# Seven products of half blocks for five channel groups of a gated mixer, projection B ahead of A, gate rows behind the heads

## The chip, the cores and the metric

The kernel runs on one core of a Trainium2 chip as one launch. The metric is device time in microseconds, the median of several runs. Engines are named as in the profile: PE or TensorE (matmuls), PEld (its weight loads), DVE or VectorE, ACT or ScalarE, POOL or GpSimd, SP or SyncE (which issues nearly all DMAs).

## The reference: one step of a hybrid decoder layer

One layer for 1024 prompt rows and 8 sample rows, D = 1024, all in float32. Cut to what matters:

```python
mod = silu(c) @ ada_w + ada_b
shift, scale, gate = split(mod, 3)
h = rmsnorm(x, norm_pre) * (1 + scale) + shift
proj = h @ w_in                                   # 10256 columns
hA, cA, bA, zA, qkv, zB, beta, alpha, gA, gB = split(proj)
a_conv, new_buf_a = causal_dwconv(cA * hA, buf_a, conv_a_w)      # width 3
yA = ((bA * a_conv) * silu(zA)) @ w_out_a
q, k, v = split(silu(causal_dwconv(qkv, buf_b, conv_b_w)))       # width 4, then l2norm of q, k
o, S = gated_delta_chunked(q, k, v, sigmoid(beta), g(alpha), s0) # 8 heads of 128
yB = (rmsnorm(o, onorm_w) * silu(zB)) @ w_out_b
merged = sigmoid(gA) * yA + sigmoid(gB) * yB
y = x + gate * rmsnorm(merged @ w_o, norm_post)
```

The outputs are y for both groups of rows, the last rows of both convolutions and the delta-rule states.

## The kernel before

Activations lie transposed: channels on the 128 partitions, 1032 tokens (`NT`: 1024 of the prompt, 8 of the samples) along the free dimension. Every float32 operand of a large matmul is split into a rounded high part and the remainder (type float32r), and a product is three matmuls: high x high, high x low, low x high. The input h lies in `xh` and `xl` (128 x 8 x 1032 each) from the start to the end of the input projection.

The work of TensorE is an ordered list, `jobs`. A job makes 128 output channels for all tokens: three groups of 344 tokens (`GROUPS`), each 8 k-tiles of three matmuls into one PSUM bank, so 72 matmuls. The job's weights are loaded two jobs ahead (`w_load`, 512 KB on SP) and split one job ahead (`w_split`: two casts on ScalarE, two subtractions on VectorE). After each group `evac` empties the bank. The order of the list before: for each of 8 heads the jobs k, q, v, up to two gate jobs and z; then for each of 8 channel groups of branch A the jobs h, c, b, z (`branch_a_jobs`); two late gate jobs; 8 jobs of projection A (`w_out_a`), 8 of projection B (`w_out_b`). Behind the list comes the tail, `merged @ w_o` with norm and residual by 128 rows.

Everything else (the delta rule of a head, the sample rows, the gate rows, loads and splits for the projections) is written as generators, "strands". A planner of its own, `Sched`, adds up planned costs of every instruction on each engine while the program is written. `slot()`, called after every k-tile, lets each strand take its next step once its planned time and a slack of 450 ns (`SLK`) have been reached by TensorE's planned clock; `force(cond)` moves that clock on and lets strands step until `cond` holds. The planner thereby fixes the order of instructions in each engine's queue and nothing else: on the chip every queue runs in order and waits on semaphores.

Names that the change touches:

- `rowgate_gen`: the `gate` part of the modulation, by 8 column blocks of 128: load, cast, remainder, 16 matmuls. It is started ahead of job 3, so in the heads, and holds three of the five buffers `T4`.
- `T4`, `MT` (`Slots`): numbered buffers, taken and given back first in, first out.
- `yAsc`, `yBsc`, `gAsc`, `gBsc`: DRAM scratch for the branch outputs and the gates.
- `to_outputs`, before the fourth channel group: waits for all strands, releases the heads' pool `bp`, and loads and splits the first three yA rows (`load_split`); later groups write their split output straight into `ya`.
- `to_out_a`, `to_out_b`: at the start of the projections `xh`, `xl` are released, `mrg`, `yb` and `wo` allocated, loads started.

The hooks that tie these together:

```python
hook(3, lambda: start(rowgate_gen()))
hook(iga + 4 * GRP_SW, to_outputs)
hook(ioa, to_out_a)
hook(iob, to_out_b)
```

## Time and profile before

| | |
|---|---|
| median of 3 runs | 1485.18 us (1481.81 to 1486.23) |
| the profiled execution | 1483.92 us, its span 1482.2 us |
| mean granted TensorE clock | 0.987 |
| busy share of the span: PE, DVE, ACT, POOL | 98%, 57%, 41%, 2% |
| instructions | 24892, of them 9890 matmuls |
| DMA | 133.14 MB, mean 90 GB/s |

All instructions are recorded by a helper, so every row of the profile has the line L121; groups are told apart by tile names (`pm_t<-xh,whi` is a matmul of the job list into PSUM, `pa_t` a small matmul of a strand, `wlo<-wraw,whi` a weight remainder). Matmuls overlap in the record, so a matmul's cost is the distance of starts. Groups of rows stand by engine, operation, tiles and shape with count, busy us and mean ns of one, and behind the bar the idle time of the engine just before and who ended it.

### The profile page before, as it was taken

Reading aid. Unit: us, or ns where it says so; the run is one execution under the profiler, and the core shown is the slowest. Engines: PE = TensorE matmul, PEld = TensorE weight load, DVE = VectorE, ACT = ScalarE, POOL = GpSimd, SP = SyncE. Lnnn points to the kernel's source line nnn. Section 1 sums busy time; section 2 is a strip of 40 time slices with the busy share of each in tenths; the row PEclk is TensorE's granted clock in tenths of the full one; section 3 lists DMA queues with packets and bytes.
Section 4 is the critical chain, followed back from the end, with each engine's and each line's share of the span. In section 5 each row is a group of like instructions: output and inputs, shape, how many; then the busy total and the mean of one; then the engine's idle time right before and its main releaser. Section 6 shows DMA issues by size and latency. Waiting matters only on the chain.

```text
span 1482.2 us, 24892 instructions
## 1 busy us (share of the span) xinstructions
PE 1448.8 (98%) x9890; PEld 1392.2 (94%) x9890; DVE 838.5 (57%) x2244; ACT 614.0 (41%) x1480; POOL 32.1 (2%) x59
## 2 busy tenths in 40 slices
PE   7999999999999999999999999999999999999997
PEld 4899999889999999999999999999999999999786
DVE  6755955957849677596765853432332342353454
ACT  6766543662835736367464223211111252131221
POOL 0000000000100000000000000000000000000000
PEclk9999998999999999999999999999999999999999
DMA  9523332233332323223232221411121174250222
GB/s 324 139 60 90 90 93 79 86 87 75 109 79 60 94 80 93 79 60 97 78 95 60 67 51 43 131 44 43 46 55 43 58 249 151 71 157 29 88 86 72
DMA packets 178250, 133.14 MB, mean 90 GB/s; under 512 B 23284, under 2 KB 164197, under 8 KB 178124
## 3 DMA queue, kind: packets, MB, share of 16 engines
q1 hardware_dynamic: 177930, 131.45, 30.4%
q8 instruction: 78, 1.28, 0.3%
q14 instruction: 40, 0.33, 0.1%
q10 hardware_dynamic: 202, 0.08, 0.0%
HBM read 105.95 MB, written 25.78 MB: 89 GB/s over the span
## 4 chain that ended last, share of the span: by engine, by line
PE 86%; DVE 6%; DMA 4%; ACT 2%; issue 1%; SPq 0%; DVEq 0%; ACTq 0%
PE pm_t L121 72%; PE pa_t L121 12%; PE pb L121 2%; DVE kq L121 1%; DMA gcB<-gsc 1%; DVE Ttmp L121 1%; DVE Tt L121 1%; DMA Tn<-sT 1%; DMA xs<-in_x_prompt_dram 1%; DMA At<-sA 1%; SPq L121 0%; ACT DA L121 0%; ACT L121 0%; DVE wlo L121 0%; DVE vT L121 0%
## 5 line engine op out<-in xcount | busy, mean ns | idle before, releaser
L121 PE MATMUL pm_t<-xh,whi 128*128 128x344 f32 x1896 | 631.8, 333 | 0.0
L121 PE MATMUL pm_t<-xl,whi 128*128 128x344 f32 x1896 | 611.0, 322 | 0.0
L121 PE MATMUL pm_t<-xh,wlo 128*128 128x344 f32 x1896 | 610.9, 322 | 0.0
L121 PEld LDWEIGHTS pm_t<-xh,whi 128*128 128x128 f32 x1896 | 360.7, 190 | 1.6
L121 PEld LDWEIGHTS pm_t<-xl,whi 128*128 128x128 f32 x1896 | 360.3, 190 | 0.2
L121 PEld LDWEIGHTS pm_t<-xh,wlo 128*128 128x128 f32 x1896 | 359.9, 190 | 0.3
L121 ACT CAST whi<-wraw 128x512 fp32r<-128x512 f32 x192 | 115.1, 623 | 250.5 <-PE pm_t L121 249.4
L121 DVE TENSOR_TENSOR wlo<-wraw,whi 128x512 fp32r<-128x512 f32 x192 | 129.2, 685 | 151.0 <-ACT whi L121 150.4
L121 PE MATMUL pm_t<-ya,whi 128*128 128x344 f32 x384 | 90.8, 320 | 0.0
L121 PE MATMUL pm_t<-yb,whi 128*128 128x344 f32 x384 | 90.5, 320 | 0.0
L121 DVE TENSOR_TENSOR Ttmp<-At,Tt 32x31 f32<-32x31 f32 (+15 forms) x248 | 81.4, 328 | 11.0 <-DMA At<-sA 5.9
L121 DVE TENSOR_TENSOR Tt<-Tt,Ttmp 32x31 f32<-32x31 f32 (+15 forms) x248 | 81.6, 329 | 4.9
L121 PE MATMUL pm_t<-wo,mh 128*128 128x512 f32 x256 | 80.5, 396 | 0.0
L121 DVE SCALAR_TENSOR_TENSOR kq<-raw,vecs,kq 128x528 f32<-128x528 f32 x96 | 70.9, 757 | 1.4 <-ACT kq L121 1.2
L121 PEld LDWEIGHTS pm_t<-ya,whi 128*128 128x128 f32 x384 | 66.2, 188 | 0.0
L121 PEld LDWEIGHTS pm_t<-yb,whi 128*128 128x128 f32 x384 | 66.2, 188 | 0.0
L121 PE MATMUL pm_t<-ya,wlo 128*128 128x344 f32 x192 | 61.4, 320 | 0.0
L121 PE MATMUL pm_t<-yb,wlo 128*128 128x344 f32 x192 | 61.3, 319 | 0.0
L121 PEld LDWEIGHTS pm_t<-wo,mh 128*128 128x128 f32 x256 | 48.1, 188 | 11.7
L121 ACT COPY vn<-pa_t 128x128 f32<-128x128 f32 x64 | 16.9, 264 | 97.3 <-PE pa_t L121 97.1
L121 ACT ACTIVATE junk<-pa_t 128x128 f32<-128x128 f32 x192 | 53.7, 280 | 5.1 <-PE pa_t L121 2.4
L121 ACT ACT_TABLE_LOAD x35 | 44.9, 1283 | 18.2 <-DVE kq L121 10.0
(323 smaller groups left out, 1874.9 us busy)
## 6 DMA issues: line engine op xcount, KB each, us to landing
wraw<-in_w_in_dram SPq DMA_DIRECT2D x80, 512.0 KB
aw<-in_ada_w_dram SPq DMA_DIRECT2D x16, 512.0 KB
gBsc<-gate SPq DMA_DIRECT2D x8, 516.0 KB
gAsc<-gate SPq DMA_DIRECT2D x8, 516.0 KB
mrg<-gAsc SPq DMA_DIRECT2D x8, 516.0 KB
sg<-gBsc SPq DMA_DIRECT2D x8, 516.0 KB
xs<-in_x_prompt_dram SPq DMA_DIRECT2D x8, 512.0 KB
rg_raw<-in_ada_w_dram SPq DMA_DIRECT2D x8, 512.0 KB
```

Of the source, the lines that this page charges most:

```text
L121: r = f(*args, **kw)
```

## The change

For a pair of output tiles (h and c, or b and z of one channel group) the weights are seen as 2 x 2 blocks (output tile by half of the 1024 input channels) and x as 2 x 2 blocks (half of the channels by half of the tokens). Instead of eight block products, seven are made of sums of blocks (Winograd's form of Strassen's product). A product has 4 k-tiles and two halves of 258 tokens (`PW`) for both pairs: 48 matmuls of 258 columns.

- Channel groups 3 to 7 of branch A leave the job list: `products()` runs 5 x 7 products after job `isp`, with all eight PSUM banks. Groups 0 to 2 stay jobs.
- `quarter_gen`, started with the first heads, makes the sums of x blocks on VectorE, splits them and stores them in DRAM (`txs`); `block_load` loads them from POOL's queue when the products begin, three blocks into slots and one over a quarter of `xh`, `xl`.
- `weight_load` and `weight_gen` load the weight halves and make their sums and splits, at most one product ahead. `finish_group` does the convolution and the gating of a group, then stores it to `yAsc`.
- PSUM is added into four accumulators in SBUF (28 additions of 258 and 8 copies per group).
- The gate jobs all stand in the heads, two per head.
- `bp` is released at the entry of the products and replaced by 28 slots of 128 x 1032 (`L[0]`), 7 more come when `xh`, `xl` are released. The later stages take their buffers from these.
- Projection B comes before A. Both read their rows from DRAM row by row (`load_rows`), and job 0 of a projection has the planner make each row's instructions before the matmul that needs it (`Rows`, `force`).
- `rowgate_gen` starts with projection B and works in three blocks of 344, 344 and 336 columns, one k-tile of 128 rows at a time.

The diff, cut to its core:

```diff
-GRP_SW = 3
-N_LATE = 2
+HT = NT // 2
+PW = HT // 2
+NSL, NSR = 28, 7
+SG = 3
+RG = ((0, 344), (344, 344), (688, 336))
...
+    txs = dram.tile([2, 2, 4, P, NT], F32R, name="txs")
...
                 for k in range(NK):
+                    if isinstance(rh, Rows):
+                        force(lambda: k in rh.rows)
                     PE.matmul(ps[:n, :gn], lhsT=hi[:, k, :n], rhs=rh[:, k, g0:g0 + gn], start=k == 0, stop=False)
...
     def rowgate_gen():
+        for c0, n in RG:
             pt = ps_aux()
             for k in range(NK):
+                yield from when(lambda: slots().ready(2))
+                r_, v_ = slots().get("rg_r", NT), slots().get("rg", NT)
+                raw, hi, lo = r_[:, 0:n], v_[:, 0:n].bitcast(F32R), v_[:, GW:GW + n].bitcast(F32R)
+                SY.dma_start(out=raw, in_=ada_w[0, k * P:(k + 1) * P, 2 * D + c0:2 * D + c0 + n])
+                yield
+                A.copy(out=hi, in_=raw)
+                yield
+                tt(lo, raw, hi.bitcast(F32), ALU.subtract)
+                yield
+                PE.matmul(pt[:64, 0:n], lhsT=cP[:, k, :], rhs=hi, start=k == 0, stop=False)
+                PE.matmul(pt[:64, 0:n], lhsT=cP[:, k, :], rhs=lo, start=False, stop=k == NK - 1)
...
+    def quarter_gen():
+        for k in range(4):
+            yield from when(lambda: T4.ready(2))
+            a, b = T4.get("qa", NT), T4.get("qb", NT)
+            a1, a2, b1, b2 = a[:, 0:HT], a[:, HT:NT], b[:, 0:HT], b[:, HT:NT]
+            tt(a, xh[:, k, :].bitcast(F32), xl[:, k, :].bitcast(F32), ALU.add)
+            yield
+            tt(b, xh[:, 4 + k, :].bitcast(F32), xl[:, 4 + k, :].bitcast(F32), ALU.add)
+            yield
+            tt(a1, a2, a1, ALU.subtract)
+            tt(a2, b2, a2, ALU.subtract)
+            yield
+            tt(b2, b2, a1, ALU.subtract)
+            tt(b1, b1, b2, ALU.subtract)
+            yield
+            for r, v in enumerate((a, b)):
+                yield from when(lambda: T4.ready(2))
+                hi, lo = T4.get("qhi", NT), T4.get("qlo", NT)
+                A.copy(out=hi.bitcast(F32R), in_=v)
+                yield
+                tt(lo.bitcast(F32R), v, hi, ALU.subtract)
+                T4.give(v)
+                store(txs[r, 0, k].bitcast(F32), hi)
+                store(txs[r, 1, k].bitcast(F32), lo)
+                T4.give(hi)
+                T4.give(lo)
+                yield
...
-        for g in gates[2 * h:min(2 * h + 2, len(gates) - N_LATE)]:
+        for g in gates[2 * h:2 * h + 2]:
             gate_job(*g)
         zb_job(h, st_h)
-    hook(3, lambda: start(rowgate_gen()))
...
+    PROD = ("P1", "P2", "P6", "P7", "P4", "P5", "P3")
...
+    def weight_gen(raw):
+        n = 0
...
+        for t in range(SG, NK):
+            a11, a12, a21, a22 = ((t, o, hf) for o in range(2) for hf in range(2))
+            for p in PROD:
+                src = {"P1": a11, "P2": a12, "P6": a11, "P7": a21, "P4": a22, "P5": None, "P3": a12}[p]
+                yield from when(lambda: unit[0] >= n - 1, lambda: src is None or src in raw)
+                hi_ = wpool.tile([P, NK, P], F32R, tag="whi", name="whi", bufs=2)
+                lo_ = wpool.tile([P, NK, P], F32R, tag="wlo", name="wlo", bufs=2)
...
+                A.copy(out=hi, in_=v)
+                yield
+                tt(lo, v, hi.bitcast(F32), ALU.subtract)
+                made[t, p] = (hi_, lo_)
+                n += 1
+                yield
+                if p == "P2":
+                    yield from when(lambda: a22 in raw and a21 in raw)
...
+                    tt(sum_, raw[a21], raw[a22], ALU.add)
+                    yield
+                    tt(raw[a21], raw[a11], raw[a21], ALU.subtract)
+                    tt(raw[a11], sum_, raw[a11], ALU.subtract)
+                    yield
+                    tt(raw[a12], raw[a12], raw[a11], ALU.subtract)
+                elif p in ("P6", "P7", "P4", "P3"):
+                    drop(src)
+
+    def block_load():
+        for b, r, cs in (("T2", 1, slice(HT, NT)), ("T3", 0, slice(HT, NT)), ("T4", 1, slice(0, HT))):
+            yield from when(lambda: L, lambda: L[0].ready(4))
+            blocks[b] = parts = []
+            for part in range(2):
+                for kk in (0, 2):
+                    v = L[0].get("tx", NT)
+                    parts.append(v)
+                    GP.dma_start(out=v.rearrange("p (k n) -> p k n", k=2).bitcast(F32R),
+                                 in_=txs[r, part, kk:kk + 2, :, cs].rearrange("k p n -> p k n"))
+            yield
+        for part, x_ in enumerate((xh, xl)):
+            GP.dma_start(out=x_[:, 0:4, HT:NT], in_=txs[0, part, :, :, 0:HT].rearrange("k p n -> p k n"))
+        blocks["T1"] = True
...
+    def finish_group(t, tiles):
+        h, c, b, z = tiles
+        tt(c, c, h, ALU.mult)
+        yield
+        act(h, c, AF.Copy, scale=tap_a(t, 2))
...
+        for w in (1, 0):
+            d = 2 - w
+            stt(h[:, d:S], c[:, 0:S - d], tap_a(t, w), h[:, d:S], ALU.mult, ALU.add)
+            stt(h[:, S:NT], hv[:, :, w], tap_a(t, w), h[:, S:NT], ALU.mult, ALU.add)
+            yield
+        L[0].give(c)
+        tt(h, h, b, ALU.mult)
+        L[0].give(b)
+        act(z, z, AF.Silu)
+        yield
+        tt(h, h, z, ALU.mult)
+        store(yAsc[t], h)
...
+    def products():
+        force(lambda: all(e.gen in kept for e in bg))
         bp.release()
+        L.append(Slots(alloc("m", "left"), "sl", NSL, NT))
+        start(block_load())
+        banks = [ps_main() for _ in range(4)] + [ps_aux() for _ in range(4)]
+        n = 0
+        for t in range(SG, NK):
+            tiles = [L[0].take("acc", NT) for _ in range(4)]
+            for p in PROD:
+                blk = {"P6": "T2", "P7": "T3", "P4": "T4", "P5": "T1"}.get(p)
+                force(lambda: (t, p) in made and (blk is None or blk in blocks))
+                unit[0] += 1
+                whi, wlo = made.pop((t, p))
+                if t == NK - 1:
+                    if p == "P7":
+                        start(load_rows("yb", yBsc))
...
+                for q in range(2):
+                    ta, tb = tiles[2 * q:2 * q + 2]
+                    for half in range(2):
+                        ps = banks[4 * (n % 2) + 2 * q + half]
+                        for k in range(4):
+                            xh_, xl_ = operand(p, k, half)
+                            PE.matmul(ps[:, :PW], lhsT=whi[:, 4 * q + k, :], rhs=xh_, start=k == 0, stop=False)
+                            PE.matmul(ps[:, :PW], lhsT=whi[:, 4 * q + k, :], rhs=xl_, start=False, stop=False)
+                            PE.matmul(ps[:, :PW], lhsT=wlo[:, 4 * q + k, :], rhs=xh_, start=False, stop=k == 3)
+                            if k < 3:
+                                slot()
...
+                        if p == "P1":
+                            A.copy(out=C11, in_=v)
+                            A.copy(out=C12, in_=v)
+                        for out, in_ in {"P1": (), "P2": ((C11, C11),), "P6": ((C12, C12),), "P7": ((C22, C12),),
+                                         "P4": ((C21, C22),), "P5": ((C22, C22), (C12, C12)),
+                                         "P3": ((C12, C12),)}[p]:
+                            tt(out, v, in_, ALU.add)
+                        slot()
...
+            start(finish_group(t, tiles))
...
+    def load_rows(key, ysc):
+        for k in range(NK):
+            yield from when(lambda: L[0].ready(3))
+            raw, hi, lo = (L[0].get(n_, NT) for n_ in ("yraw", "yhi", "ylo"))
+            SY.dma_start(out=raw, in_=ysc[k])
+            yield
+            A.copy(out=hi.bitcast(F32R), in_=raw)
+            yield
+            tt(lo.bitcast(F32R), raw, hi, ALU.subtract)
+            L[0].give(raw)
+            rows[key][k] = (hi.bitcast(F32R), lo.bitcast(F32R))
+            held[key] += [hi, lo]
+            yield
...
+    def to_out_b():
+        xpool.release()
+        T["mrg"] = alloc("mrg", "right").tile([P, NK, NT], F32, name="mrg")
+        L[0].extend(alloc("m2", "right"), "sr", NSR)
+        start(rowgate_gen())
+        start(conv_state_gen("a"))
...
+    hook(iob + 2, lambda: start(load_rows("ya", yAsc)))
...
+    hook(ioa + 1, lambda: start(wo_gen()))
...
     start(ba_gen())
-    run(jobs, 1)
-    drain_bg()
+    start(quarter_gen())
+    run(jobs, 1, isp)
+    products()
+    run(jobs, isp, len(jobs))
+    force(lambda: all(("wo", t) in T for t in range(NK)))
```

More of the change, by code (lines that the diff above doesn't have):

```diff
@@ L650, in give, with __init__, __getitem__, when @@
             self.free.append(self.held.pop(id(v))[0])
-        def grow(self, pool, n):
-            self.more, self.n = pool, len(self.free)
-            assert not self.held
-            self.free += list(range(self.n, self.n + n))
-        def shrink(self):
-            assert not self.held
-            self.free = list(range(self.n))
-            self.more.release()
+    class Rows:
+        def __init__(self, rows, part):
+            self.rows, self.part = rows, part
+        def __getitem__(self, i):
+            return self.rows[i[1]][self.part][i[0], i[2]]
+    def when(*conds):
+        while not all(c() for c in conds):
+            yield
     wq = {}
@@ L683, in w_split, with run @@
                 tt(e[2][:, ks, :n], e[0][:, ks, :n], e[1][:, ks, :n].bitcast(F32), ALU.subtract)
-    def run(jobs, first):
-        for i in range(first, len(jobs)):
+    def run(jobs, first, stop):
+        for i in range(first, stop):
             w_ap, c0, n, src, before, evac, after = jobs[i]
@@ new lines, in rowgate_gen @@
+                slots().give(v_)
+                slots().give(r_)
+            yield from when(lambda: slots().ready())
+            v_ = slots().get("rg_g", NT)
+            g, ab, npw = (v_[:9, i * GW:i * GW + n] for i in range(3))
+            SY.dma_start(out=ab, in_=ada_b[:, 2 * D + c0:2 * D + c0 + n].to_broadcast([9, n]))
+            SY.dma_start(out=npw, in_=norm_post[:, c0:c0 + n].to_broadcast([9, n]))
+            yield
+            A.copy(out=g, in_=pt[32:41, 0:n])
+            tt(g, g, pt[0:9, 0:n], ALU.add)
@@ L1404, in sig_gen, with drop_rows @@
+    rows, held = {"ya": {}, "yb": {}}, {"ya": [], "yb": []}
+    def drop_rows(key):
+        for v in held[key]:
+            L[0].give(v)
     def sig_gen(dst, src):
```

251 lines of the change are left out of this document (128 added, 123 removed).

## The prediction

> **What bounds the kernel now.** I read the page first (busy shares, clock, chain), then stretches between job boundaries, then TensorE's timeline where it is not dense, then the groups of instructions by shape for prices.
>
> ```profile
> span 1482.2 us, 24892 instructions
> PE 1448.8 (98%) x9890; PEld 1392.2 (94%) x9890; DVE 838.5 (57%) x2244; ACT 614.0 (41%) x1480; POOL 32.1 (2%) x59
> GB/s 324 139 60 90 90 93 79 86 87 75 109 79 60 94 80 93 79 60 97 78 95 60 67 51 43 131 44 43 46 55 43 58 249 151 71 157 29 88 86 72
> PE 86%; DVE 6%; DMA 4%; ACT 2%; issue 1%; SPq 0%; DVEq 0%; ACTq 0%
> ```
>
> TensorE carries 86% of the chain. The stretches (us, then busy us and counts of each engine, granted clock, DMA share, GB/s) say where it has no slack at all; the rows of 3.4 us are for later.
>
> ```profile
> core 0: us, PE busy (x) PEld busy (x) DVE busy (x) ACT busy (x) POOL busy (x), PEclk, DMA share, GB/s
> 60.00:130.00 70.00, 66.44 (x450) 63.29 (x449) 38.90 (x90) 47.52 (x105) 0.62 (x3) 1.00 0.32 86
> 968.90:1195.10 226.20, 226.20 (x1441) 226.20 (x1441) 70.03 (x121) 41.52 (x77) 0.00 (x0) 1.00 0.20 54
> 1195.10:1376.90 181.80, 181.80 (x1160) 181.53 (x1159) 73.55 (x123) 52.70 (x67) 0.00 (x0) 1.00 0.38 126
> 157.60:161.00 3.40, 3.22 (x12) 3.25 (x13) 3.40 (x10) 0.00 (x0) 0.00 (x0) 0.51 0.59 154
> 280.50:283.90 3.40, 3.32 (x12) 3.32 (x13) 3.40 (x8) 3.36 (x6) 0.22 (x1) 0.50 0.02 4
> ```
>
> From 968.9 to 1195.1 run 20 jobs, 1440 matmuls of 344 columns: 0.157 us each, 11.31 us a job, no gap; VectorE is busy 70 of 226 us. Columns taken out of this stretch shorten the span one for one, as long as nothing else becomes late there.
>
> **The change, part by part.**
>
> *(a) Products: fewer columns.* Five groups were 20 jobs. Now each is 7 products of 2 tile rows x 2 halves x 4 k x 3 = 48 matmuls of 258 columns: 35 x 48 = 1680. The nearest row is a run of six matmuls of 256 columns between others (start, us, operation):
>
> ```profile
> 129.57 0.28 PE L121 MATMUL pa_t<-kqh 128*128 128x256 f32 x1
> ...
> 130.28 0.32 PE L121 MATMUL pm_t<-xh,whi 128*128 128x344 f32 x1
> ```
>
> Six starts in 0.71 us: 0.118 each at 256 columns against 0.157 at 344, or 0.44 ns a column; 258 columns cost 0.119 us. A product takes 5.72 us, all 35 take 200.2: **-26.0 us** (bounds: -24 if 0.120, -28 if exactly 7/8). By the Trainium skill, "TensorE: Matmul & The Clock Gate", section "Wait — 56ns, not 53.3ns?", a warm matmul costs its columns at 2.4 GHz and about 2.5 ns, 110 ns here, which would make the 35 products 185 us; the trace's 256 columns at 118 ns are above that rule, and the sum goes by the row.
>
> Prices for the other engines (by shape: busy, mean ns | idle before):
>
> ```profile
> L121 DVE TENSOR_TENSOR wlo<-wraw,whi 128x512 fp32r<-128x512 f32 x192 | 129.2, 685 | 151.0 <-ACT whi L121 150.4
> L121 DVE SCALAR_TENSOR_TENSOR aA<-uA,vecs,aA 128x1048 f32<-128x1048 f32 x16 | 20.9, 1304 | 0.2
> L121 DVE TENSOR_TENSOR kql<-kq,kqh 128x1024 fp32r<-128x1024 f32 x16 | 19.4, 1220 | 6.4 <-ACT kqh L121 3.1 <-DMA sT<-Tt 1.9 <-DMA gBsc<-gate 1.2
> L121 DVE TENSOR_TENSOR DA<-pa_t,DA 128x256 f32<-128x256 f32 x32 | 13.2, 412 | 0.0
> L121 DVE TENSOR_TENSOR hA<-hA,szA 128x1032 f32<-128x1032 f32 x8 | 9.8, 1225 | 0.0
> L121 DVE TENSOR_TENSOR rg_lo<-rg_raw,rg_hi 128x1024 fp32r<-128x1024 f32 x8 | 9.7, 1213 | 0.2 <-ACT rg_hi L121 0.2
> L121 ACT CAST yb<-yst 128x1032 fp32r<-128x1032 f32 x8 | 8.3, 1050 | 2.3 <-DMA yst<-yBsc 2.1 <-DVE yst L121 0.3
> L121 ACT ACTIVATE mrg<-mrg 128x1032 f32<-128x1032 f32 x8 | 8.5, 1067 | 9.2 <-DMA mrg<-gAsc 9.2
> L121 ACT ACT_TABLE_LOAD x35 | 44.9, 1283 | 18.2 <-DVE kq L121 10.0 <-DVE vT L121 4.7 <-DVE ban L121 1.6
> ```
>
> *(b) VectorE in the products.* Per group: 7 weight remainders and 4 weight sums of 1024 (11 x 1.22 = 13.4), 28 additions out of PSUM of 258 (28 x 0.41 = 11.5), finish_group with three full-width products and two multiply-adds (3 x 1.23 + 2 x 1.30 = 6.3): 31 us of the 40 that TensorE needs. The mean fits; the order does not. finish_group of group t-1 starts together with product P1 of group t, and weight_gen makes P2's remainder and all four sums only then, because it may run one product ahead. P6 is due after two products, and its third matmul needs the remainder: at 11.45 + 0.24 = 11.7 us. In the order in which the planner's slots take the two strands in turn, VectorE has before it: P3's last bank 0.41, c*h 1.23, P2's remainder 1.22, sum 1.22, multiply-add 1.30, two differences 2.44, multiply-add 1.30, two banks of P2 0.82, the last difference 1.22, a bank 0.41, h*b 1.23, the last bank 0.41, P6's remainder 1.22: 14.4 us. TensorE then waits 2.7 us in each of groups 4 to 7. Bounds: 0.2 us if the second multiply-add and h*b fall behind the remainder, 3.5 with the few-column pieces counted. I take the written order: 4 x 2.7 = 11.
>
> Such a wait has a second price. TensorE's waits in the heads (idle time and releaser in brackets):
>
> ```profile
> 114.38 0.66 PE L121 MATMUL pa_t<-ident,kq 128*128 128x128 f32 x4 [2.50 <-DVE kd L121]
> 157.78 0.37 PE L121 MATMUL pa_t<-ident,sm_r 128*8 128x128 f32 x1 [2.73 <-DVE sm_r L121]
> 280.58 0.37 PE L121 MATMUL pa_t<-rg_hi,cP 128*64 128x128 f32 x1 [2.25 <-ACT rg_hi L121]
> ```
>
> After the second and the third the granted clock was 0.51 and 0.50 over 3.4 us (rows above), 1.7 us lost; after the first nothing. So 0 to 1.7 us per wait, and I take 1.2: **+16 us** for (b). By the Trainium skill, same page, section "HAM oscillation — how this bites in real kernels", the clock falls only after gaps of more than some 3.4 us; the trace disagrees, half clock follows 2.25 us. By that rule (b) would be 11.
>
> *(c) Entry into the products.* bp is released, the new slots lie over it, and the second half of group 3's weights is loaded only then. A similar release in the kernel before:
>
> ```profile
> 948.82 0.32 SPq L121 DMA_DIRECT2D yAsc<-hA  x1
> 951.91 1.27 SPq L121 DMA_DIRECT2D yst<-yAsc  x3
> 951.93 0.45 ACT L121 COPY hA<-pm_t 128x344 f32<-128x344 f32 x1 [4.13 <-DMA yAsc<-hA]
> 955.40 1.06 ACT L121 CAST ya<-yst 128x1032 fp32r<-128x1032 f32 x1 [0.94 <-DMA yst<-yAsc]
> 956.67 1.06 ACT L121 CAST ya<-yst 128x1032 fp32r<-128x1032 f32 x1 [0.22 <-DMA yst<-yAsc]
> ```
>
> The last store was issued 2.5 us after the job's end (946.3, two jobs before 968.9) and held the slots to 951.9; a load takes 3.5 us to its use, the next in line 1.3 more. So the two halves land 5.6 + 4.8 = 10.4 us in, three sums, the last difference and the remainder take 6.1, P6 starts at 16.5, 4.8 late. Bounds 0 (slots free at once: 10.9) and 8 (beside the block loads). Taken: **+5**. The blocks: POOL loads 8.4 MB, beside 2.1 MB of weights; at the 324 GB/s of the page's first slice all is there after 32 us, P5 is due at 28.6 + 5. No wait taken, up to 12 at lower rates.
>
> *(d) Entry into projection B.* load_rows takes one row after the other: load, cast, remainder, in planner time some 7 us a row, and starts four products (23 us) before the end. So three of eight rows are queued by then, and job 0 forces the others out between finish_group of the last group, the gate's sigmoid and the first gate rows. SP comes to rows 5 to 7 only after the store of yA[7], which waits for c*h 1.23, a scale 1.05, two multiply-adds 2.60, h*b 1.23, sigmoid and silu with a table load each (2 x 2.35, half beside VectorE) and the last product 1.23, about 11 us with a row's remainder between. Then 3.5 to the first row, 2 x 1.3 to row 7, cast 1.05, remainder 1.23: 19.4 us, where TensorE wants it after 7 x 0.47 = 3.3. That is 16 us of wait, of which the gate rows' and transposes' matmuls fill about 2, and 1.7 of half clock after it: **+15**. Bounds: 3 (the rows' loads run ahead of everything, VectorE alone limits, rows partly done) to 20. Before, projection A was entered without a gap (the row 1195.10:1376.90).
>
> *(e) Gate rows behind the heads.* The matmuls come to the same (128 of 128 columns against 48 of 344). In the heads TensorE waited for rg_hi 2.25 us, with 1.7 of half clock behind it: **-4** (bounds 0, if the next wait takes its place, and -5). In projection B the same chain runs beside dense matmuls on engines busy 73.55 and 52.70 of 181.80 us: 0. Two gate jobs move into head 7, as many jobs as before.
>
> *(f) Sums of x, in the first heads.* Four rounds of four operations at 1.23 and four half-wide at 0.69 are 31 us of VectorE, 8 casts 8.4 of ScalarE; rowgate_gen leaves 8 x 1.21 there. Between 60 and 130 us VectorE is idle 31 us. Sixteen stores (8.4 MB) on SP add 120 GB/s to 86. Cover is TensorE's 66.44 of 70 us; it also takes four of the five T4 slots, where the gate rows took three. Bounds -5 to +10, taken **+2**.
>
> *(g) Projection A, wo, tail:* ya's rows start six jobs (68 us) ahead, wo seven; the tail's matmuls are unchanged. 0, at most +3.
>
> **Sum:** -26 + 16 + 5 + 15 - 4 + 2 = +8 us. The profiled execution took 1483.9 us, 1.3 below the median of 1485.2; on the median: **1493 us**.
>
> **The rivals.**
>
> *R1, the waits are mostly hidden* (the other side). Place: P6 in each group and the first job of B. If VectorE's order is kinder by two operations, (b) is 4 x 0.2 to 1, no clock loss; (c) 2; and if the rows' loads are not behind the store, (d) is 6. Sum -26 + 3 + 2 + 6 - 4 + 2 = -17: 1468. It decides once (b) + (c) + (d) are under 28 us instead of 36. For it: SP and ScalarE ran ahead of TensorE in the rows at 951.9. Against: VectorE's 14.4 us are in order.
>
> *R2, a narrower matmul costs as much as a wide one:* 1680 x 0.157 = 264, 38 us more than 226; with the waits 1557. The run at 256 columns speaks against it.
>
> *R3, the first heads become late:* the 31 us of (f) hit a VectorE with 31 us free, and heads 0 and 1 hold the buffers that head 2's jobs wait for; +10: 1503. Against: the gate rows leave.
>
> *R4, the blocks come late:* the loads come from POOL, of which no row exists; at the 1186 us slice's 249 GB/s, 10.5 MB take 42 us, P5 waits 9: 1502. The Trainium skill, "SBUF — State Buffer", section "Who interferes with whom", says that VectorE's two-port operations hold up a DMA issued from GpSimd; no run here shows it.
>
> **How the numbers follow.** My forecast 0.53 (own range 1483 to 1506), R1 0.30, R2 0.02, R3 0.08, R4 0.07. A measurement tells about 0.3% (4.5 us) from no change: under 1480.7 faster, over 1489.6 slower. R1 gives 0.28 faster; of the forecast 0.03 is faster, 0.10 the same, 0.40 slower; R3, R4 and R2 are slower. Faster 0.31, same 0.12, slower 0.57. The range takes in R1 and R3, R4 with some of their spread: 1464 to 1509.
>
> **What would show it.** After: 35 products whose matmuls stand 0.119 us apart; TensorE waits of 2 to 3 us for wlo at P6, four times, with half clock behind; 10 us and more at the first job of B for yhi or ylo; no wait for rg_hi in the heads. Wrong it is if those waits are under 1 us, or if the heads end later than 946 + 23 us.

## The result and the profile after

The changed kernel takes 1495.3 us (1490.3 to 1498.7), where the kernel before took 1483.7 on the same chip: a ratio of 1.0076, 95% interval 1.0055 to 1.0097. The forecast was 1493. The size of the sum is right by luck, since most of its terms are not: two that were forecast at 31 us together cost hardly anything, and two that were forecast at 7 us together cost about 50.

The head of the page of the changed kernel, with its chain of waits (the engines' shares):

```profile
span 1494.6 us, 25637 instructions
PE 1423.4 (95%) x10050; PEld 1362.3 (91%) x10050; DVE 947.8 (63%) x2391; ACT 645.1 (43%) x1512; POOL 42.0 (3%) x73
PE 75%; DVE 10%; DMA 7%; ACT 4%; SPq 2%; issue 2%; DVEq 0%; ACTq 0%
```

TensorE is busy 25 us less than before and the span is 12.4 us longer: what was taken out of it came back as waits, and its share of the chain fell from 86% to 75%. Stretches of the changed kernel between the starts of jobs (the columns are those of the prediction's stretches) say where:

```profile
core 0: us, PE busy (x) PEld busy (x) DVE busy (x) ACT busy (x) POOL busy (x), PEclk, DMA share, GB/s
185.00:210.00 25.00, 7.90 (x40) 7.61 (x39) 19.57 (x65) 3.34 (x6) 0.00 (x0) 0.62 0.28 75
972.60:1034.90 62.30, 43.07 (x338) 42.54 (x338) 30.51 (x47) 11.24 (x18) 8.52 (x13) 0.84 0.80 229
1034.90:1196.70 161.80, 161.20 (x1345) 161.03 (x1344) 118.93 (x194) 54.26 (x78) 0.00 (x0) 1.00 0.27 83
1196.70:1214.70 18.00, 16.17 (x93) 15.03 (x94) 16.30 (x27) 12.06 (x18) 0.00 (x0) 0.91 0.73 234
```

The first row lies in the second head, the next two are group 3 and groups 4 to 7 of the products, the last is the first job of projection B. Two rows have a TensorE that is not dense: 7.90 us of work in 25, and 43.07 in 62.30. Both holes stand at the top of its waits (engine and what it waited for: us in total, times, longest); the third row here is its one wait at the entry of projection B:

```profile
PE pm_t L122 <- ACT whi L122: 18.0, 1, 18.0
PE pm_t L122 <- ACT gate L122: 17.1, 1, 17.1
PE pm_t L122 <- DVE ylo L122: 1.8, 1, 1.8
```

**The hole in the heads.** Timeline rows of VectorE, ScalarE and TensorE around it (start, us, operation, idle time before it and who ended that):

```profile
171.13 1.22 DVE L122 TENSOR_TENSOR qa<-xh,xl 128x1032 f32<-128x1032 f32 x1
172.27 1.22 DVE L122 TENSOR_TENSOR qb<-xh,xl 128x1032 f32<-128x1032 f32 x1
173.65 1.20 ACT L122 ACTIVATE vT<-raw,vecs 128x1056 f32<-128x1056 f32 x1
205.71 1.14 ACT L122 COPY gate<-pm_t 128x344 f32<-128x344 f32 x3 [19.36 <-DVE Ttmp L122]
206.21 0.65 PE L122 MATMUL pm_t<-xh,whi 128*128 128x344 f32 x1 [17.10 <-ACT gate L122]
207.98 1.05 ACT L122 CAST qhi<-qa 128x1032 fp32r<-128x1032 f32 x1 [1.13 <-DMA sT<-Tt]
```

The two sums `qa` and `qb` are made at 171 us and their split begins only at 208: two of the five T4 buffers stand full of waiting data. `vT` takes another at 173.65, and `At` and `Tt` of head 0's inversion loop (`Ttmp` is its scratch) hold the last two until the loop ends at 205.7. The gate job of head 1 has no buffer to be copied to, PSUM stays full, and TensorE stands still.

**The hole at the entry of the products**, in rows of POOL, SP, VectorE and TensorE:

```profile
976.12 0.34 SPq L122 DMA_DIRECT2D yAsc<-hA  x1
981.10 24.76 SPq L122 DMA_DIRECT2D wr<-in_w_in_dram  x11
981.84 4.93 POOL L122 DMA_DIRECT2D tx<-txs  x7 [9.18 <-DMA yAsc<-hA]
997.13 1.23 DVE L122 TENSOR_TENSOR wsum<-wr 128x1024 f32<-128x1024 f32 x1 [13.78 <-DMA wr<-in_w_in_dram]
1002.26 1.22 DVE L122 TENSOR_TENSOR wlo<-wq,whi 128x1024 fp32r<-128x1024 f32 x1
1002.26 1.42 PE L122 MATMUL pm_t<-tx,whi 128*128 128x258 f32 x5 [18.02 <-ACT whi L122]
```

The store of the last branch output holds the slots until 981.1. Then SP's weight loads and POOL's block loads start side by side; the weights a21 and a22 (1 MB) are used 16.0 us after their issue, the sums take 5 more, and P6 begins 18.2 us late.

**Where the span went.** Each profiled execution, cut at the first matmul of the products, of the first projection and of the tail. The first column holds 60 jobs of one size in every kernel; in the kernel before, two of them are of group 3 of branch A, and two gate jobs stand in the second column instead.

| profiled execution | heads and groups 0-2 | products (before: 20 jobs) | projections | tail |
|---|---|---|---|---|
| before | 968.9 | 226.3 | 182.1 | 105.0 |
| after | 972.6 | 224.1 | 193.6 | 104.3 |
| difference | +3.7 | -2.2 | +11.5 | -0.7 |

### The profile page after: what moved, and what is told of

Its sections match the earlier page's. It is cut to its first block, busy times and chain, and to the rows that moved or that the text cites. A ratio compares the mean times of both kernels' runs of the same rounds, so it can differ in the third digit from the quotient of the medians.

```text
span 1494.6 us, 25637 instructions
## 1 busy us (share of the span) xinstructions
PE 1423.4 (95%) x10050; PEld 1362.3 (91%) x10050; DVE 947.8 (63%) x2391; ACT 645.1 (43%) x1512; POOL 42.0 (3%) x73
## 4 chain that ended last, share of the span: by engine, by line
PE 75%; DVE 10%; DMA 7%; ACT 4%; SPq 2%; issue 2%; DVEq 0%; ACTq 0%
PE pm_t L122 57%; PE pa_t L122 16%; SPq L122 2%; DVE kq L122 2%; DMA gcB<-gsc 2%; PE pb L122 2%; DVE Tt L122 2%; DVE Ttmp L122 2%; DVE wlo L122 1%; DMA xs<-in_x_prompt_dram 1%; ACT junk L122 1%; DMA aw<-in_ada_w_dram 1%; ACT L122 1%; DMA txs<-qlo 1%; DVE vT L122 1%
## 5 line engine op out<-in xcount | busy, mean ns | idle before, releaser
L122 PE MATMUL pm_t<-xh,whi 128*128 128x344 f32 (+1 forms) x1576 | 520.6, 330 | 18.8 <-ACT gate L122 17.1
L122 PE MATMUL pm_t<-xh,wlo 128*128 128x344 f32 (+1 forms) x1576 | 500.7, 318 | 0.6 <-DVE wlo L122 0.6
L122 PE MATMUL pm_t<-xl,whi 128*128 128x344 f32 (+1 forms) x1576 | 499.8, 317 | 0.0
L122 PEld LDWEIGHTS pm_t<-xh,wlo 128*128 128x128 f32 x1576 | 297.9, 189 | 1.1 <-DVE wlo L122 0.9
L122 PE MATMUL pm_t<-ylo,whi 128*128 128x344 f32 x384 | 123.4, 321 | 1.8 <-DVE ylo L122 1.8
L122 PE MATMUL pm_t<-yhi,whi 128*128 128x344 f32 x384 | 123.2, 322 | 0.6 <-DVE acc L122 0.6
L122 PE MATMUL pm_t<-yhi,wlo 128*128 128x344 f32 x384 | 123.6, 322 | 0.0
L122 PEld LDWEIGHTS pm_t<-ylo,whi 128*128 128x128 f32 x384 | 72.6, 189 | 2.2 <-DVE ylo L122 2.1
L122 PEld LDWEIGHTS pm_t<-yhi,whi 128*128 128x128 f32 x384 | 72.7, 190 | 1.2 <-issue 0.8
L122 PEld LDWEIGHTS pm_t<-yhi,wlo 128*128 128x128 f32 x384 | 72.6, 189 | 0.0
L122 PEld LDWEIGHTS pm_t<-tx,whi 128*128 128x128 f32 x256 | 41.1, 197 | 18.2 <-issue 18.2
## 6 DMA issues: line engine op xcount, KB each, us to landing
tx<-txs POOLq DMA_DIRECT2D x12, 516.0 KB, 12.4
```

The source lines that it names most:

```text
L122: r = f(*args, **kw)
```

## The experiments

The theory was that the loss is two waits, one for a T4 buffer (H) and one for loads that land in the wrong order (E1), and a price of the gate rows that depends on their place (G). Ratios are to the kernel before on the same chip, with 95% intervals; the differences in us are to the changed kernel's 1495.3.

**1. Sums of x two heads later** (`sums_from_head2`)

```diff
+        if h == 2:
+            hook(i0, lambda: start(quarter_gen()))
...
-    start(quarter_gen())
     run(jobs, 1, isp)
```

> quarter_gen is started with head 2 instead of head 0; nothing else changes. Theory H (the sums of x crowd the five T4 buffers in the heads, and head 1's gate job waits 17.3 us for one): the 17.3 us wait near 189 us and the half clock behind it (about 2 us) go, heads 0 and 1 lose some 3 us of smaller waits too, and 4 to 8 us come back in heads 2 to 4: about 1495 - 19 + 6 = 1482 us. Rival H2 (the buffers are short in every head alike): the wait moves to head 3 with about its size, 1490 to 1497. Rival H3 (the wait is the planner's order, not the buffers): the wait near 189 us stays.

Measured: 1537.7 us, ratio 1.0352 (1.0325 to 1.0379), 42 us slower than the change. TensorE's waits of this kernel:

```profile
PE pm_t L122 <- ACT raw L122: 15.7, 2, 10.1
PE pm_t L122 <- ACT gate L122: 14.5, 1, 14.5
```

The wait near 189 us is gone, as H had it, but others of 10.4, 14.7, 10.2 and 5.8 us stand at 278, 305, 595 and 706 us, and the 60 jobs end at 1017.7 instead of 972.6. H2 is nearest in kind (the buffers are short in later heads too), yet its 1490 to 1497 is 41 us off and H's 1482 is 56. Added up over TensorE's trace from 60 us to the products, the heads have 25 us more of waits than in the change and 21 us more lost to half clock. By the source, more strands want the five buffers in later heads; which of them lost one to the sums wasn't followed up.

**2. Three buffers instead of four** (`sums_three_buffers`)

```diff
-                yield from when(lambda: T4.ready(2))
-                hi, lo = T4.get("qhi", NT), T4.get("qlo", NT)
+                yield from when(lambda: T4.ready())
+                hi = T4.get("qhi", NT)
...
-                tt(lo.bitcast(F32R), v, hi, ALU.subtract)
+                tt(v.bitcast(F32R), v, hi, ALU.subtract)
```

> quarter_gen writes each remainder over the sum it came from, so it holds at most three T4 buffers instead of four (two sums, one high part); it still starts with head 0. Theory H (buffers): one buffer more is free, the wait near 189 us falls from 17.3 us to under 5, quarter_gen ends earlier than 342 us: 1478 to 1485 us. Rival H3 (planner's order): the wait stays within 3 us of its size, 1492 to 1498.

Measured: 1494.0 us, ratio 1.0056 (1.0037 to 1.0075): nothing. Rows of VectorE and ScalarE:

```profile
181.19 1.26 DVE L122 TENSOR_TENSOR qa<-xh,xl 128x1032 f32<-128x1032 f32 x1 [0.16 <-DMA txs<-qhi]
182.43 1.24 DVE L122 TENSOR_TENSOR qb<-xh,xl 128x1032 f32<-128x1032 f32 x1
209.31 1.14 ACT L122 COPY gate<-pm_t 128x344 f32<-128x344 f32 x3 [22.53 <-DVE Ttmp L122]
211.62 1.05 ACT L122 CAST qhi<-qa 128x1032 fp32r<-128x1032 f32 x1 [1.16 <-DMA sT<-Tt]
```

By its number this spoke for H3, the planner's order. The rows say otherwise: what was saved is the remainder's buffer, and at the moment that counts it is not the remainder that holds buffers but the two sums waiting for their split, 181 to 211 us. The edit missed the suspect.

**3. Sums in chunks, one buffer at rest** (`sums_in_chunks`). One buffer takes the four sums of 258 columns.

```diff
-            a, b = T4.get("qa", NT), T4.get("qb", NT)
+            for o in (0, PW):
...
+                v = T4.get("qa", 4 * PW)
...
+                tt(v.bitcast(F32R), v, hi, ALU.subtract)
```

> quarter_gen goes in eight rounds of half the columns, all four sums of a round in one T4 buffer and each remainder written over its sum: it holds one buffer between rounds and two at most, from head 0 on as in the change; the same sums, 32 stores of half the size. Theory H (two sums wait in two of the five buffers while the inversion loop holds two and the next v one, so head 1's gate job has none): the wait near 189 us, 17.3 us and 20.4 with three buffers, falls under 5 us, and the first heads end 14 to 20 us earlier: 1474 to 1482 us. Rival H3 (the order in the queues, not a buffer): the wait stays over 12 us, 1490 or more. Rival H4 (the first heads are short of VectorE, as 31 us of sums in a VectorE with 31 us free): the wait goes, but comes back as small ones, over 1486.

Measured: 1471.2 us, ratio 0.9916 (0.9889 to 0.9944), 24 us faster than the change and below H's range. The same 25 us stretch as above:

```profile
185.00:210.00 25.00, 22.04 (x136) 21.73 (x135) 16.97 (x56) 7.54 (x23) 1.09 (x2) 0.95 0.43 122
```

and, in TensorE's waits, the one for a gate that is left (in a later head, at 275 us):

```profile
PE pm_t L122 <- ACT gate L122: 4.6, 1, 4.6
```

TensorE works 22.04 of the 25 us instead of 7.90. The 60 jobs end at 945.8, 26.8 us earlier, and the products and projections stay as they were (225.3 and 192.4). It is the same arithmetic on the same engines. The edit changes the order of the steps too, but so did experiment 2, which left two full buffers waiting and kept the wait: the buffers were the cost. H3 falls; H4 too, since VectorE's 31 us of sums are all still there.

**4. Weights ahead of the release** (`weights_before_release`)

```diff
+                elif t == SG:
+                    v = E.get("wr", D)
...
+    E = Slots(tc.alloc_tile_pool(name="early", bufs=1, side="left"), "e", 2, CW)
...
-    raws = [bp.tile([P, CW], F32, name=f"raw{i}") for i in range(2)]
+    raws = [E.get("raw", CW) for i in range(2)]
```

> The two weight tiles a21 and a22 of group 3 go into the two buffers that the heads' convolutions used (raws, now in a pool of their own, not in bp), so they are loaded two jobs ahead and do not wait for bp's release; the later slots stay 28 in all. The TensorE wait of 18.2 us at the third product is then set by block T2 alone. Theory E1 (the wait is the weights' landing beside the block loads, 16 us after issue): T2's four loads are issued at 981.8 us, the first loads of the queue land in some 6 to 8 us: P6 starts at 989 instead of 1002 and the wait is 4 to 6 us; the time falls 12 to 14 us, to 1481 to 1483. Rival E2 (all loads of this stretch are held by the same bandwidth and T2 lands as late as the weights did): P6 starts at 995 to 1000, the time falls 2 to 7 us.

Measured: 1494.7 us, ratio 1.0063 (1.0039 to 1.0087), no gain. The waits of TensorE at the third and the fifth product, and VectorE's rows before the last of them:

```profile
988.30 0.72 PE L122 MATMUL pm_t<-tx,whi 128*128 128x258 f32 x4 [3.13 <-DVE wlo L122]
991.79 0.58 PE L122 MATMUL pm_t<-tx,whi 128*128 128x258 f32 x1 [2.78 <-DMA tx<-txs]
1011.30 0.55 PE L122 MATMUL pm_t<-tx,whi 128*128 128x258 f32 x1 [6.11 <-issue]
1009.63 1.23 DVE L122 TENSOR_TENSOR wsum<-wr 128x1024 f32<-128x1024 f32 x1 [22.25 <-DMA wr<-in_w_in_dram]
1010.78 0.42 DVE L122 TENSOR_TENSOR acc<-pm_t,acc 128x258 f32<-128x258 f32 x1
```

P6 does start at 988.3, as E1 said, but then it waits for its block, half clock follows, and P4 waits 6.1 us. The profile names no releaser for that, but VectorE's rows show one: the sum of group 4's weights stands at the head of its queue and waits 22.25 us for their load, and the additions that empty P6's PSUM banks stand behind it. P4 uses the same banks, by the source, and starts at 1011.30, when the first addition has ended (1010.78 and 0.42). Group 3 takes 60.4 us against 62.3. Neither theory holds: E1 has P6's start but not the gain; E2 has neither P6's start nor the gain, and the late loads that it had in mind are only a part. Taking away one late load showed the next, and one of them held up a queue in which other work stood behind it.

**5. Blocks behind the weights on one queue** (`blocks_behind_weights`)

```diff
-            yield from when(lambda: L, lambda: L[0].ready(4))
+            yield from when(lambda: L, lambda: L[0].ready(4), lambda: (SG, 1, 1) in got)
...
-                    GP.dma_start(out=v...
+                    SY.dma_start(out=v...
```

> The twelve block loads go to SP's queue behind the loads of a21 and a22, instead of POOL's queue beside them; nothing else changes. Theory E1 (contention): a21 and a22 (1 MB) land some 4 to 5 us after 981.1, the sums take 6 us behind them, T2 (2.1 MB) lands at about 992: P6 starts at 992 to 993 instead of 1002.3, the wait falls from 18.2 to 8 or 9 us and the time to 1485 to 1487. Rival E3 (release of the slots and the sums' chain set it, 5.6 + 4.8 + 6.1 us as forecast, and the contention is no part): nothing gained over 2 us. Rival E4: T3 and T4 now come late, since SP has group 4's weights between them, and P7 or P4 waits what P6 no longer does: within 3 us of 1495.

Measured: 1485.0 us, ratio 1.0005 (0.9988 to 1.0021), 10 us faster than the change. SP's queue and VectorE's first sum:

```profile
979.59 2.52 SPq L122 DMA_DIRECT2D wr<-in_w_in_dram  x4
982.15 2.13 SPq L122 DMA_DIRECT2D tx<-txs  x4
986.37 1.23 DVE L122 TENSOR_TENSOR wsum<-wr 128x1024 f32<-128x1024 f32 x1 [4.48 <-DMA wr<-in_w_in_dram]
```

The weights are used 6.8 us after issue instead of 16.0, P6 starts 8.9 us late instead of 18.2, and no later product of the group waits 2 us. E1 holds with its numbers; E3 and E4 fall. The bytes are the same; their order differs, and the blocks are issued by SP instead of POOL. Which of the two counts isn't shown, since the same order on POOL's queue wasn't run.

**6. Gate rows in head 4** (`gate_rows_in_head4`). The line taken away is that of `to_out_b`.

```diff
+        if h == 4:
+            hook(i0, lambda: start(rowgate_gen()))
...
-        start(rowgate_gen())
```

> rowgate_gen is started with head 4, behind the sums of x, instead of with projection B; it takes its buffers from T4 as before the change. Theory G (the gate rows in B cost their matmuls, 48 x 0.157 = 7.5 us, and in the heads the same matmuls plus the waits for the five buffers): the jobs of B fall from 11.95 to 11.34 us, B and A together by 7 to 9 us, and the heads grow by 10 to 30 us: 1498 to 1518. Rival G2 (in the heads they fill waits that are there anyway): the heads grow by under 5 us: 1488 to 1492.

Measured: 1514.2 us, ratio 1.0208 (1.0191 to 1.0226), G's range. The projections fall from 193.6 to 182.6 us and the 60 jobs end 24.8 us later.

**7. Gate rows in the first heads again** (`gate_rows_in_first_heads`, on top of 3)

```diff
+    hook(3, lambda: start(rowgate_gen()))
...
-        start(rowgate_gen())
```

> On top of the sums in chunks (1471.2 us): rowgate_gen is started ahead of job 3, where it stood before the change, in its new form of 24 small steps of two buffers. It prices step (e) where the change made it. Theory G (behind the heads the gate rows cost 11 us, measured as 193.6 against 182.6 us for projections B and A; in the first heads their matmuls plus the buffers they hold cost twice that): the projections fall by 10 to 11 us, the heads (945.8 us to the products) grow by 18 to 30: 1479 to 1491 us. Rival G2 (the -23 us that separate the heads of sums_in_chunks from those of before, 968.9, come from the order of the gate jobs and not from the gate rows): the heads grow by under 8 us and the time falls to 1463 to 1469. Rival G3 (they cost in the heads what they cost behind them): within 4 us of 1471.

Measured: 1492.0 us, ratio 1.0043 (1.0019 to 1.0067), so 20.8 us above the same kernel with the gate rows behind the heads, and just over G's range. The stretch of its projections:

```profile
1205.80:1388.50 182.70, 182.70 (x1163) 182.39 (x1162) 79.31 (x128) 55.11 (x69) 0.00 (x0) 1.00 0.39 129
```

They take 182.7 us against 192.4, and the 60 jobs end at 979.8 against 945.8: the gate rows cost 9.7 us behind the heads and 34.0 in them, where G had 18 to 30. G2 and G3 fall.

**8. A late remainder** (`late_remainder`)

```diff
                     tt(raw[a12], raw[a12], raw[a11], ALU.subtract)
+                    if t > SG:
+                        for _ in range(5):
+                            tt(raw[a11], raw[a11], raw[a11], ALU.max)
```

> The change, and in groups 4 to 7 five more VectorE operations of 1024 columns (a maximum of the tile with itself, 1.14 us from start to start) between the weight sum and P6's remainder: they put on VectorE what the forecast of term (b) believed to be there. In the queue the remainder then stands behind P2's last addition, one more of the five, h*b and a difference. Theory M (term (b) was zero because the queue has P6's remainder 3.3 us ahead of need, and not because such a wait is hidden): TensorE waits 4 to 5 us for wlo at P6 in each of the four groups, with 1.2 to 3 us of half clock behind: +21 to +32 us, 1516 to 1527. Rival M2 (the next products make it up, with eight PSUM banks between the engines): the waits are there but the time grows by less than 10 us: under 1505.

Measured: 1521.2 us, ratio 1.0237 (1.0220 to 1.0254), 25.9 us above the change. The first of the four waits in TensorE's timeline:

```profile
1051.09 1.44 PE L122 MATMUL pa_t<-tx,whi 128*128 128x258 f32 x5 [3.65 <-ACT whi L122]
```

and the stretches behind it (the clock is the third column from the end):

```profile
1051.10:1056.10 5.00, 5.00 (x22) 4.89 (x23) 2.76 (x3) 0.89 (x1) 0.00 (x0) 0.50 0.28 109
1056.40:1059.50 3.10, 3.10 (x27) 3.10 (x27) 0.85 (x2) 0.00 (x0) 0.00 (x0) 0.98 0.00 0
```

P6's four waits are 3.8, 4.6, 4.6 and 3.8 us, and the product behind each takes 7.5 to 8.6 us instead of 5.75, since the clock is at 0.50 for 5.4 to 6.0 us of the first three and 3.4 of the last: 16.7 of waits and 10.0 of half clock make 26.7. M holds and M2 falls: nothing is made up later. So term (b) named a real mechanism with a real price; in the change the order doesn't have it.

**9. The three edits together** (`chunks_queue_early`: 3, 5 and 4)

> Three edits together: sums of x in chunks, block loads on SP's queue behind group 3's weights, and these weights loaded before bp's release. If the three are independent: -17 of the heads, -10 of the queue (measured alone), and of the 8.9 us wait that was left 3 to 5 more, since only T2 (2.1 MB at 350 GB/s, 6 us after the slots come free) is then in front of P6: 1495 - 17 - 10 - 4 = 1464, range 1460 to 1470. If bandwidth sets the entry (about 7.3 MB must land from 981 on, at 350 GB/s 21 us), the third edit gives nothing, since its 1 MB is then only replaced by group 4's: 1468 to 1472.

Measured: 1456.6 us, ratio 0.9810 (0.9795 to 0.9825), under both ranges. Products: 211.3 us, against 224.1 in the change and 213.1 with the queue alone. Early weights gave nothing by themselves and a little here, where they are no longer beside the blocks; the rest of the gain over the forecast is the chunks' 24 instead of 17.

**10. The last two gate jobs behind group 2** (`chunks_queue_early_late_gates`, on top of 9)

```diff
-        for g in gates[2 * h:2 * h + 2]:
+        for g in gates[2 * h:min(2 * h + 2, 14)]:
...
+    for g in gates[14:]:
+        gate_job(*g)
```

> As the run before, and the last two gate jobs of head 7 stand behind group 2, as the last two jobs ahead of the products. Their last instructions before the release are a copy out of PSUM and a store, where group 2 had silu, a product and a store: theory R (the release of bp waits for the last store): P6's wait falls by another 2 to 3 us, and head 7 ends 0 to 3 us earlier: 1460 to 1464 us. Rival: the store itself is slow beside T1's loads (5.0 us, 976.1 to 981.1, against 3.1 us before the change), so that only 1 us comes back: within 2 us of the run before.

Measured: 1463.2 us, ratio 0.9852 (0.9827 to 0.9877), 6.6 slower than run 9. The products are 1.9 us shorter, where R had 2 to 3 for P6's wait, but the heads end 4.4 us later (953.5 against 949.1), for a reason no theory had: the clock, told below.

**11. P5 third in group 3** (`p5_third`, on top of 9)

```diff
+    PROD0 = ("P1", "P2", "P5", "P6", "P7", "P4", "P3")
+    order = lambda t: PROD0 if t == SG else PROD
...
+                            if p == "P5":
+                                A.copy(out=C22, in_=v)
+                            else:
+                                tt(C21, v, C12, ALU.add)
+                                tt(C12, C12, C22, ALU.add)
+                                tt(C22, C22, C21, ALU.add)
```

> On top of the three edits (sums in chunks, blocks on SP's queue behind the weights, weights before the release; 1456.6 us): in group 3 alone P5, whose block T1 is loaded before the release, is computed third and P6 fourth; its result goes into the free accumulator and is added in at P7. Theory E5 (P6's entry waits only for T2, which is complete 5.9 us after P6 would start, at 966.9 against 961.0): P6 is due 5.75 us later, so the waits of 3.5 and 2.3 us and about 3 us of half clock behind them go, 8 to 9 us: 1447 to 1450. Rival E6 (the accumulators come with the same release, and P5 needs P1's banks emptied into them): P5 waits instead, 2 to 4 us, and half the gain stays out: 1451 to 1455.

Measured: 1450.4 us, ratio 0.9765 (0.9750 to 0.9780), at the edge of E5's range. Group 3 and the groups behind it:

```profile
947.40:990.40 43.00, 41.25 (x339) 40.54 (x338) 25.70 (x40) 12.39 (x21) 0.07 (x1) 1.00 1.01 308
990.40:1151.80 161.40, 161.28 (x1347) 161.11 (x1345) 121.47 (x197) 54.78 (x78) 0.00 (x0) 1.00 0.27 83
```

The entry costs 43.0 us where four dense groups average 40.35: 2.7 us are left of 22. The change with three edits and this order is 2.4% faster than the kernel before and 3.0% faster than the change.

## Why the prediction was right and wrong

The total came out because errors of opposite sign cancelled, which is luck. By the prediction's own steps:

- **(a) Columns, -26.0: right.** Starts of 258-column matmuls stand 0.120 us apart, the prediction's lower bound of the gain; 35 products of 5.75 us are 201.3 us, -25.0.
- **(b) P6 waits for its remainder, +16: wrong, it is 0.** Groups 4 to 7 are dense (the row 1034.90:1196.70). The step that failed is "in the order in which the planner's slots take the two strands in turn": the order of the written generators was taken for the order of the queue. VectorE's timeline of the changed kernel, from group 4's last product (P3) to group 5's P6, which begins at 1086.6:

```profile
1069.79 1.23 DVE L122 TENSOR_TENSOR wsum<-wr 128x1024 f32<-128x1024 f32 x1 [0.94 <-DMA wr<-in_w_in_dram]
1071.60 1.22 DVE L122 TENSOR_TENSOR wlo<-wr,whi 128x1024 fp32r<-128x1024 f32 x1
1073.41 1.21 DVE L122 TENSOR_TENSOR wr<-wsum,wr 128x1024 f32<-128x1024 f32 x1
1076.49 1.22 DVE L122 TENSOR_TENSOR wlo<-wr,whi 128x1024 fp32r<-128x1024 f32 x1
1080.29 1.22 DVE L122 TENSOR_TENSOR wr<-wr 128x1024 f32<-128x1024 f32 x1
1082.57 1.22 DVE L122 TENSOR_TENSOR wlo<-wr,whi 128x1024 fp32r<-128x1024 f32 x1
```

  The weight sum stands ahead of P1's remainder, where the generator writes it behind P2's. The sums need only the loaded weights, and the assembled program has them as early as that; so P6's remainder (the last row) is done 8.7 us after P1's start instead of 14.4. The sentence that the planner fixes each queue's order is therefore true only of dependent instructions. Experiment 8 gives the price that the forecast would have had to pay, and experiment 4 the price of such an early place: a sum whose weights are late holds up what stands behind it.
- **(c) Entry into the products, +5: the largest miss at the entry, +22.8** (224.1 less 201.3). The steps were each named (release 5.6, loads 4.8, sums and remainder 6.1); they took 8.5, 16.0 and 5.1, so P6 came 18.2 us late, and half clock and a small wait behind it make the rest. What failed is above all the load of 4.8 us, taken from rows where SP loads alone; beside 6.3 MB of blocks it was 16.0. The prediction had named that case in its bound of 8; it was nearly three times that. No product of the change waits for a block, which is what R4 was about. Experiments 4, 5 and 11 show what makes this term: 22.8 in the change, 20.6 with early weights alone, 11.8 with one queue, 3.1 with all three edits and the block that is there first used first.
- **(d) Entry into projection B, +15: nearly nothing.** The first job takes 17.97 us, but with the gate rows elsewhere it takes 12.2 (experiments 6 and 7), as the first job of projection A did in the kernel before (12.2). So it is the gate rows that make it long, by 5.8 us. The last row is indeed late, though its load doesn't wait for the store of yA[7] (at 1206.62):

```profile
1203.34 0.35 SPq L122 DMA_DIRECT2D yraw<-yBsc  x1
1208.39 2.37 DVE L122 TENSOR_TENSOR ylo<-yraw,yhi 128x1032 fp32r<-128x1032 f32 x2
```

  Its remainder is done 14.1 us after the start, where the forecast had 19.4. The step that failed is the need, 3.3 us after the start: in TensorE's queue the other tokens' matmuls with the first seven rows stand ahead of those with the last, where the job is written group by group: from 1203.8 to 1210.3 it works on without a wait, and before that it waits once, 1.8 us. This is the error of (b) again, the written order taken for the order of a queue.
- **(e) Gate rows behind the heads, -4: the direction is right, the size is not.** Behind the heads they cost 9.7 us (experiment 7) to 11.0 (experiment 6), where the forecast said 0; in the first heads 34.0, in head 4 beside the wide sums 24.8. The mis-sized term is the heads' price: it was read from the one wait named rg_hi with 1.7 us of half clock. Added up over TensorE's trace from 60 us to the products, the 34.0 are 14.0 of waits, 10.7 lost to half clock and 9.3 of more work (their 48 matmuls are 7.5 at 0.157). The 23.1 us between the kernel before and experiment 3 (968.9 less 945.8) are not all theirs: 13.7 are lost to half clock, and in the kernel before this stands behind no wait at two places, the second 400 us after the last matmul of the gate rows (390.6):

```profile
236.10:246.40 10.30, 10.30 (x55) 9.69 (x53) 2.97 (x12) 1.86 (x4) 0.00 (x0) 0.50 0.18 51
792.50:799.40 6.90, 6.90 (x39) 6.04 (x38) 1.19 (x4) 0.72 (x2) 0.00 (x0) 0.51 0.09 31
```

- **(f) Sums of x in the first heads, +2: +26.8** (972.6 less 945.8), the price of the wide form over the one in chunks: 18.5 of waits, 4.7 of half clock and some 3.6 that neither explains. R3 had the place and a size of 10, but put it on VectorE's time. The text does say that the sums take four of the five T4 buffers, and charges nothing for that: this is the step that failed.
- **(g) Projection A, tail, 0:** the tail is 0.7 shorter; projection A has no wait, and its gate rows are counted in (e).

So +3.7 in the heads is -23.1 + 26.8; -2.2 in the products is -25.0 + 22.8; +11.5 in the projections is 11.0 of gate rows (by experiment 6) and 0.5 of the rest; with the tail's -0.7 that is, but for rounding, the 12.4 us by which the span grew. Of the prediction's own tests, both rows for what would make it wrong came true (waits at P6 under 1 us, heads that end later than 969: 972.6) while the total held.

What stays open: what each of the single waits of experiment 1 waited for; how the 23.1 us divide between the gate rows and the half clock that came without them; whether the order alone, on POOL's queue, does what experiment 5 did. The price of the gate rows in their old form, with no sums beside them, wasn't tried.

## What to carry to other kernels

Work that is spread into a stage with spare engine time is not free if it holds buffers while it waits: count who holds each buffer at the moment when a dependent loop holds the rest, and make the unit that waits small. When a stage starts with more bytes than its first steps can wait for, put the loads in one queue in order of need, and use first what is there first. Do not read a queue's order out of the source; look at the assembled order or a trace, above all where an instruction depends on little.

## What the runs showed of the hardware

- **Two queues together loaded at some 354 GB/s.** Stretches of the changed kernel at the entry, with SP's and POOL's loads side by side:

```profile
990.00:995.00 5.00, 0.00 (x0) 0.00 (x0) 0.00 (x0) 0.00 (x0) 2.00 (x3) 0.50 1.21 354
995.00:1000.00 5.00, 0.00 (x0) 0.00 (x0) 2.84 (x4) 0.00 (x0) 0.72 (x1) 0.50 1.21 353
```

  The Trainium skill, "DMA: Bandwidth & Descriptors", section "Where 436 GB/s comes from", states some 358 GB/s for transfers from HBM; these stretches agree. In experiment 5, with all these loads on SP's queue, the same 5 us have 386 and 361, so it is no upper limit here. The forecast had used 324 in (c) and 249 in R4, means of slices of 37 us.
- **Half clock comes in pieces of 3.4 us, and the length of one wait doesn't say how many.** In the thirteen traces, every stretch at 0.50 from 60 us on lasts 3.4 us or a whole multiple of it, up to 23.9. At the four waits of 3.8 to 4.6 us of experiment 8 it is 6.8 three times and 3.4 once, which cost 1.8 to 2.9 us behind the wait. A wait of 1.55 us (experiment 1, at 569.4) had 6.8 us of half clock with it, one of 2.97 (experiment 2, at 135.6) had none. The Trainium skill, "TensorE: Matmul & The Clock Gate", section "HAM oscillation — how this bites in real kernels", has 1.67 us at half clock behind each wait of its example, of which half is lost; the stretches here are longer.
- **The clock can fall with no wait at all.** Stretches of run 10, in head 7:

```profile
770.00:772.00 2.00, 2.00 (x40) 1.75 (x40) 0.00 (x0) 0.50 (x2) 0.00 (x0) 1.00 0.00 0
774.00:776.00 2.00, 2.00 (x15) 1.94 (x13) 0.62 (x4) 0.37 (x1) 0.00 (x0) 0.50 0.00 0
```

  TensorE is recorded as busy throughout, but from 769.2 to 772.7 nearly all of its matmuls are the delta rule's 32x32 ones and the sample rows' of two columns; the clock is 0.50 from 773.1 to 786.8. In run 9, where the jobs around these are others, the stretch 775 to 785 has 1.00. The two stretches of the kernel before under (e) stand behind a run of the same tiny matmuls, those of 64x64 among them. So half clock has followed a dense run of tiny matmuls; that they are its cause, and whether by their size or their form, is not shown.
